# Attention: two triangles of weights added and transposed as one

## The chip, the cores and the metric

The kernel runs on one core of a Trainium2 chip. The core has a matmul engine (TensorE, PE in the profile, with its weight loads as PEld), a vector engine (VectorE, DVE), a scalar engine (ScalarE, ACT), a general one (GpSimd, POOL) and SyncE (SP), which issues nearly all DMAs here. Each takes its instructions in order and they meet through semaphores. SBUF is the working memory and PSUM the banks into which TensorE accumulates. The metric is device time of one execution, in microseconds (us).

## The reference

Two layers of a hybrid decoder over 512 tokens of width 1024, all in fp32. Each layer normalises its input, makes one projection (queries, keys and values for attention; queries, keys, values and a gate for retention; two output gates), runs sliding-window attention and chunkwise retention side by side, merges both through the gates, projects, adds, and then does the same with an MLP (squared ReLU, width 4096). The part that matters:

```python
C = WINDOW                       # 128
kk, vv = band(kb), band(vb)      # the block of keys before, and the block itself
s = einsum('bnqhgd,bnkhd->bnhgqk', qb, kk) * HEAD_DIM ** -0.5
rel = (arange(C)[:, None] + C) - arange(2 * C)[None, :]
valid = (rel >= 0) & (rel < WINDOW)
s = where(valid & first, s, -inf)
p = softmax(concatenate([s, sink], -1), -1)[..., :-1]
o = einsum('bnhgqk,bnkhd->bnqhgd', p, vv)
```

There are 8 query heads in 2 groups, one group to each of 2 key-value heads. A block of 128 queries sees 256 keys. Query i sees key j of the block before only if j > i, and key j of its own block only if j <= i. So the weights that are not zero fill a strict upper triangle of the first 128x128 block and the lower triangle with the diagonal of the second: together exactly one full square. The first query block has no block before it.

## The kernel before

**Products.** Every fp32 operand of a large product is split into a high and a low part, each in a form that TensorE multiplies at full rate (fp32r), and a product is three matmuls: high by high, high by low, low by high (`products`, L297 to L299). The split is a copy on ScalarE and a subtraction on VectorE: L252 and L253 for weights, `split` (L304, L305) for everything else. Weights come by DMA as 128x1024 units in the order of use (L193); `unit` sees to it that while unit i is multiplied, i+1 and i+2 are being split, with three buffers for the parts. A unit is 24 matmuls of 512 columns.

**Order.** The code is traced in program order; a planner then places each engine's instructions in an order of its own by its own costs of instructions and its own times at which they are ready, and gives out the buffers. So program order is a priority, not the order in the queues, and the queues are fixed before the kernel runs.

**Attention** is a generator that runs in the background: `chunk` calls `advance` twice per unit, which does 0.8 of a step each time while the gates, the first retention queries and keys, and the first retention gates are being projected. A step takes one query block n and one pair c of heads (one head of each group g), 16 steps per layer. In a step:
- four score matmuls into one PSUM bank, `ps` (L669): 128 queries by w keys, w = 128 for n = 0 and 256 otherwise, for two heads side by side;
- scaling, masking and the row minimum in one VectorE instruction per head (L677), from `ps` to the SBUF tile `sm` (the signs are turned, so a minimum stands for the maximum), with `nsink`, the negated sinks made once at L288, as its start; then the sink's term (L687);
- exponentials with their row sums on ScalarE (L689, L692); masked weights become zero;
- sum and reciprocal on VectorE (L693, L694), and the scaling of all w weights of each head (L696);
- `transposed` for the step of three before (the queue `pend`): a transpose by TensorE of each 128x128 block of weights into a bank `pT` (L634), four for n > 0 and two for n = 0, and a split of the bank into `p_h` and `p_l`, from which the product with values reads.

`weighted(n)` runs two steps after the last `transposed` of block n: per group, two matmuls per key block (L654, L655; tile `pv`), then the two halves are joined (L656, L657) and split. Its result is first read by the product with w_a, some tens of us after attention ends. The tiles `sm` and the rotary temporaries share six buffers; `score`, `pT`, `pv` and others share three PSUM banks; main products have five.

**Start.** SP issues the first input, inputs and weights in turn, then the table `band` (the mask of attention, L280), further weights and the rotary tables. A small tile of constants sits in front of x in the tile `little_x`.

Of the kernel before, what the change touches and what calls it, by code (L numbers as in the profile page):

```python
# [14 lines left out]
ALU = mybir.AluOpType  # L15
# [3 lines left out]
P = 128  # L19
# [7 lines left out]
N_KV = 2  # L27
# [93 lines left out]


@with_exitstack
def decoder(ctx, tc, xT, x_first, w_in, w_a, w_b, w_out, w_up, w_down, tables, decay, band, g_last, out):
    nc = tc.nc
    weights = {"w_in": w_in, "w_a": w_a, "w_b": w_b, "w_out": w_out, "w_up": w_up, "w_down": w_down}

# [17 lines left out]
    def bank(pool, name):  # L145
        return pool.tile([P, T], F32, tag=pool.name, name=name)
# [4 lines left out]
    n_gain, n_sink = 2 * DEPTH * KD, DEPTH * N_Q  # L151
    little_x = const.tile([P, P + KD * T], F32, name="x")
    gain = little_x[:, P - n_gain : P]
    sink = little_x[:, P - n_gain - n_sink : P - n_gain]
    eps, half, nsink = (little_x[:, a : a + n] for a, n in ((0, 1), (8, N_KV), (16, n_sink)))
    x = little_x[:, P:].rearrange("p (k t) -> p k t", t=T)
    xhl = const.tile([P, 2, KD, T], F32R, name="xhl")
    xh, xl = xhl[:, 0], xhl[:, 1]
# [119 lines left out]

    mask = const.tile([P, 2 * P], F32, name="mask")
    nc.sync.dma_start(mask, band)  # L280

    ident = const.tile([P, P], F32, name="ident")
    make_identity(nc, ident)
    nc.gpsimd.memset(half, 0.0)
    for g in range(N_KV):
        for b in (0, 64):
            nc.gpsimd.memset(half[b + 32 * g : b + 32 * g + 32, g : g + 1], 1.0)
    nc.vector.tensor_scalar(nsink, sink, -1.0, None, ALU.mult)  # L288


    def products(ps, pairs, start, stop, resume=False):
# [206 lines left out]
    def layer_body(layer):  # L498
# [124 lines left out]
        def attention():  # L623
            p_t = [slots.four() for _ in range(2)]
            p_h, p_l = p_t[0][0], p_t[1][0]
            pend, ready = [], []

            def transposed(n, c, sm):
                w = P if n == 0 else 2 * P
                kbs = (1,) if n == 0 else (0, 1)  # L630
                pt = bank(ps_aux, "pT")
                for i, (g, kb) in enumerate((g, kb) for g in range(N_KV) for kb in kbs):
                    at = g * w + (kb - kbs[0]) * P
                    nc.tensor.transpose(pt[:, i * P : (i + 1) * P], sm[:, at : at + P], ident)  # L634
                m = 2 * len(kbs)
                src = pt[:, : m * P].rearrange("p (i q) -> p i q", q=P)
                first = kbs[0]
                hi = p_h[:, first :: 2 if n == 0 else 1, c * P : (c + 1) * P]
                lo = p_l[:, first :: 2 if n == 0 else 1, c * P : (c + 1) * P]
                split(hi, lo, src)  # L640

            def weighted(n):
                at = slice(n * P, (n + 1) * P)
                both = big("whole")
                rest, whole = both[:, 0, :], both[:, 1, :]
                for g in range(N_KV):
                    own, other = slice(64 * g, 64 * g + 64), slice(64 - 64 * g, 128 - 64 * g)
                    po = bank(ps_aux, "pv")
                    kbs = (1,) if n == 0 else (0, 1)
                    for kb in kbs:  # L650
                        b = n - 1 + kb
                        cols = slice(b * P, (b + 1) * P)
                        p = 2 * g + kb
                        nc.tensor.matmul(po, v_both[g][:, cols], p_h[:, p, :], start=kb == kbs[0], stop=False)  # L654
                        nc.tensor.matmul(po, v_high[g][:, cols], p_l[:, p, :], start=False, stop=kb == 1)  # L655
                    nc.scalar.activation(rest[own, :], po[other, :], AF.Copy)  # L656
                    nc.vector.tensor_tensor(whole[own, :], po[own, :], rest[own, :], ALU.add)  # L657
                split(a_h[:, :, at], a_l[:, :, at], whole.rearrange("p (c q) -> p c q", q=P))

            for n in range(NB):  # L660
                w = P if n == 0 else 2 * P
                keys = slice(0, P) if n == 0 else slice((n - 1) * P, (n + 1) * P)
                at = slice(n * P, (n + 1) * P)
                for c in range(4):
                    col = layer * N_Q + 2 * c
                    ps = bank(ps_aux, "score")
                    for g in range(N_KV):
                        for i, part in enumerate((kh[g], kl[g])):
                            nc.tensor.matmul(  # L669
                                ps[:, g * w : (g + 1) * w], q_s[g][:, c, at], part[:, keys], start=i == 0, stop=i == 1  # L670
                            )
                    sm = temp("sm")
                    s3 = sm[:, : 2 * w].rearrange("p (g k) -> p g k", g=2)
                    st = small.tile([P, 8], F32, tag="st", name="st")
                    nm, es, su, rc = (st[:, 2 * i : 2 * i + 2] for i in range(4))
                    for g in range(N_KV):
                        nc.vector.tensor_tensor_reduce(  # L677
                            s3[:, g, :],
                            ps[:, g * w : (g + 1) * w],
                            mask[:, 2 * P - w :],  # L680
                            -(HEAD_DIM**-0.5),
                            nsink[:, col + g : col + g + 1],
                            ALU.add,
                            ALU.min,
                            nm[:, g : g + 1],
                        )
                    nc.vector.tensor_tensor(es, nm, sink[:, col : col + 2], ALU.add)  # L687
                    for g in range(N_KV):
                        nc.scalar.activation(  # L689
                            s3[:, g, :], s3[:, g, :], AF.Exp, bias=nm[:, g : g + 1], scale=-1.0, accum_out=su[:, g : g + 1]  # L690
                        )
                    last_exp[:] = [nc.scalar.activation(es, es, AF.Exp).ins]  # L692
                    nc.vector.tensor_tensor(rc, su, es, ALU.add)  # L693
                    nc.vector.reciprocal(rc, rc)  # L694
                    for g in range(N_KV):
                        nc.vector.tensor_scalar(s3[:, g, :], s3[:, g, :], rc[:, g : g + 1], None, ALU.mult)  # L696
                    pend.append((n, c, sm))
                    if ready and c == 1 + DELAY:
                        weighted(ready.pop())
                    if len(pend) > DEEP:  # L700
                        done = pend.pop(0)
                        transposed(*done)
                        if done[1] == 3:
                            ready.append(done[0])
                    yield
            while pend:
                transposed(*pend.pop(0))
                yield
            weighted(NB - 1)
            for t in q_t + p_t:  # L710
                slots.give(*t[1])
            slots.give(*k_s, *v_s)
# [198 lines left out]
        for u in range(4):  # L911
            hi, lo = unit("w_a", layer)
            for j in range(2):
                c = 2 * u + j
# [394 lines left out]
def _tables():  # L1309

    f = np.float32
    pos = np.arange(T, dtype=f)
    inv = np.power(10000.0, -np.arange(32) / 32).astype(f)
    ang = pos[None, :] * np.tile(inv, 4)[:, None]
    sign = np.where(np.arange(P) < 64, f(-1), f(1))[:, None]
    steps = np.append(np.arange(63, dtype=f) * (f(1) / f(63)), f(1))
    theta = f(1.0) / np.power(10000.0, steps.astype(np.float64)).astype(f)
    ang_r = pos[None, :] * np.tile(theta, 2)[:, None]
    rotary = np.stack([np.cos(ang), sign * np.sin(ang), np.cos(ang_r), sign * np.sin(ang_r)], 1).astype(f)

    log_g = np.log(1.0 - 2.0 ** (-5.0 - np.arange(RET_HEADS)))
    rel = np.arange(T)[None, :] - np.arange(P)[:, None]
    decay = np.where(rel[:, None, :] >= 0, np.exp(log_g[None, :, None] * np.maximum(rel, 0)[:, None, :]), 0.0)
    decay = (decay * RET_QK**-0.5).astype(f)

    rel = np.arange(P)[:, None] + P - np.arange(2 * P)[None, :]
    band = np.where((rel >= 0) & (rel < P), f(0), f(MASKED)).astype(f)
    return rotary, decay, band


def _laid_out(x, g_mix, w_in, sinks, w_a, w_b, w_out, g_mlp, w_up, w_down, g_final):
    r = np.arange
    wa_rows = np.concatenate([(4 * g + c) * HEAD_DIM + r(HEAD_DIM) for c in range(4) for g in range(2)])
    rotary, decay, band = _tables()
    gains = np.stack([g for l in range(DEPTH) for g in (g_mix[l], g_mlp[l])])
    heads = np.array([4 * g + c for c in range(4) for g in range(2)])
    xT = np.ascontiguousarray(x[0].T.reshape(KD, P, T).transpose(1, 0, 2))
# [11 lines left out]
        "tables": rotary,  # L1349
        "decay": decay,  # L1350
        "band": band,
        "g_last": np.ascontiguousarray(np.broadcast_to(g_final, (P, D))),
    }

# [17 lines left out]
```

## Time and profile before

| | |
|---|---|
| median of 3 runs | 1494.0 us (1493.49 to 1494.09) |
| profiled execution | 1494.36 us, of which the span from first to last instruction is 1492.6 us |
| granted TensorE clock | 0.999 |
| TensorE busy | 1485.9 us, 7212 matmuls |
| VectorE busy | 1063.4 us, 1709 instructions |
| ScalarE busy | 757.5 us, 1212 instructions |
| transposes of weights (L634) | 112, started between 61.8 and 866.0 us |

How to read it: the page of the profile gives busy time per engine, then the chain that ended last, which follows from the last instruction back to whatever released each one. A group line gives line, engine, operation, output and inputs with their shapes, count, then busy us and the mean ns of one, then the idle time of that engine ahead of them and what ended it. In a timeline the first number is the start and the second the duration, of all of a merged run together. A duration is that of one instruction from its start to its end; TensorE overlaps neighbours, so what a matmul costs the stream is the distance to the next start. Attention of layer 0 lies at about 50 to 150 us, that of layer 1 at about 785 to 880.

### The profile page before, as it was taken

How to read it: one execution, taken by the hardware profiler on the slowest of the kernel's cores; microseconds unless marked ns; L12 is line 12 of the kernel's file. 1: busy time of each engine (PE TensorE's matmuls, PEld its weight loads, DVE VectorE, ACT ScalarE, POOL GpSimd, SP SyncE). 2: the span in 40 equal slices, each digit the busy share in tenths (PEclk: the TensorE clock that was granted, in tenths of full speed). 3: DMA queues.
4: the chain of work that ended last, by engine and by line, in shares of the span. 5: the costliest groups of instructions: out<-in, count | busy, mean ns of one | idle time of the engine just before them, and what ended most of it. 6: DMA issues, size and time to landing. Idle time of an engine off the chain costs nothing.

```text
span 1492.6 us, 19003 instructions
## 1 busy us (share of the span) xinstructions
PE 1485.9 (100%) x7212; PEld 1253.3 (84%) x7212; DVE 1063.4 (71%) x1709; ACT 757.5 (51%) x1212; POOL 2.9 (0%) x13
## 2 busy tenths in 40 slices
PE   9999999999999999999999999999999999999998
PEld 7888888888888888888888888888888888888887
DVE  7877568754688787777678864687448877787763
ACT  6657355533555545444455653546326554454543
POOL 0000000000000000000000000000000000000000
PEclk9999999999999999999999999999999999999999
DMA  6422323244323332324442323232443232333341
GB/s 223 125 93 72 97 87 91 73 120 122 105 78 111 102 101 91 112 92 131 161 129 89 97 76 97 85 92 71 127 127 100 80 103 85 113 113 104 95 141 57
DMA packets 51835, 155.53 MB, mean 104 GB/s; under 512 B 6176, under 2 KB 6304, under 8 KB 51744
## 3 DMA queue, kind: packets, MB, share of 16 engines
q1 hardware_dynamic: 51456, 153.80, 33.9%
q8 instruction: 56, 0.92, 0.2%
q10 hardware_dynamic: 288, 0.52, 0.1%
q14 instruction: 35, 0.29, 0.1%
HBM read 147.48 MB, written 4.19 MB: 102 GB/s over the span
## 4 chain that ended last, share of the span: by engine, by line
PE 100%; DVE 0%; ACT 0%; issue 0%; DVEq 0%; ACTq 0%
PE mm L297 23%; PE mm L298 23%; PE mm L299 23%; PE mm L1096 11%; PE mm L1097 6%; PE rv L297 2%; PE rv L299 2%; PE rv L298 2%; PE score L669 1%; PE pT L634 1%; PE r L298 1%; PE r L299 1%; PE r L297 1%; PE pv L654 0%; PE pv L655 0%; PE ssq L394 0%
## 5 line engine op out<-in xcount | busy, mean ns | idle before, releaser
L252 ACT ACTIVATE hi<-raw 128x1024 fp32r<-128x1024 f32 (+1 forms) x314 | 316.9, 1013 | 461.4 <-PE mm L298 274.6
L253 DVE TENSOR_TENSOR lo<-raw,hi 128x1024 fp32r<-128x1024 f32 (+1 forms) x315 | 365.7, 1165 | 177.4 <-ACT hi L252 176.6
L298 PE MATMUL mm<-r,hi 128*128 128x512 f32 (+1 forms) x704 | 271.1, 385 | 0.0
L297 PE MATMUL mm<-xhl,hi 128*128 128x512 f32 (+1 forms) x696 | 269.8, 390 | 0.0
L297 PE MATMUL mm<-r,hi 128*128 128x512 f32 (+1 forms) x704 | 269.5, 386 | 0.0
L298 PE MATMUL mm<-xhl,hi 128*128 128x512 f32 (+1 forms) x696 | 268.6, 388 | 0.0
L299 PE MATMUL mm<-xhl,lo 128*128 128x512 f32 (+1 forms) x696 | 267.6, 388 | 0.0
L299 PE MATMUL mm<-r,lo 128*128 128x512 f32 (+1 forms) x704 | 266.6, 385 | 0.0
L299 PEld LDWEIGHTS mm<-r,lo 128*128 128x128 f32 x704 | 132.2, 188 | 26.6
L298 PEld LDWEIGHTS mm<-r,hi 128*128 128x128 f32 x704 | 132.3, 188 | 25.6
L297 PEld LDWEIGHTS mm<-r,hi 128*128 128x128 f32 x704 | 131.8, 188 | 26.0 <-DVE z L1075 0.3
L297 PEld LDWEIGHTS mm<-xhl,hi 128*128 128x128 f32 x696 | 131.0, 188 | 25.1 <-ACT xhl L307 0.8
L299 PEld LDWEIGHTS mm<-xhl,lo 128*128 128x128 f32 x696 | 130.9, 188 | 24.9
L298 PEld LDWEIGHTS mm<-xhl,hi 128*128 128x128 f32 x696 | 131.0, 188 | 24.3
L1096 PE MATMUL mm<-r,hi 128*128 128x512 f32 x416 | 146.8, 391 | 0.0
L1097 PE MATMUL mm<-r,lo 128*128 128x256 f32 x416 | 115.6, 278 | 0.0
L1096 PE MATMUL mm<-xhl,hi 128*128 128x512 f32 x312 | 110.5, 391 | 0.0
L1096 PEld LDWEIGHTS mm<-r,hi 128*128 128x128 f32 x416 | 78.2, 188 | 16.2
L1097 PE MATMUL mm<-xhl,lo 128*128 128x256 f32 x312 | 86.7, 278 | 0.0
L1097 PEld LDWEIGHTS mm<-r,lo 128*128 128x128 f32 x416 | 78.1, 188 | 1.8
L1096 PEld LDWEIGHTS mm<-xhl,hi 128*128 128x128 f32 x312 | 58.6, 188 | 11.8
L1097 PEld LDWEIGHTS mm<-xhl,lo 128*128 128x128 f32 x312 | 58.6, 188 | 1.7
(229 smaller groups left out, 2069.9 us busy)
## 6 DMA issues: line engine op xcount, KB each, us to landing
raw<-w_in_in SPq DMA_DIRECT2D x89, 512.0 KB, 3.6
raw<-w_down_in SPq DMA_DIRECT2D x64, 512.0 KB, 3.6
raw<-w_up_in SPq DMA_DIRECT2D x36, 512.0 KB, 3.6
raw<-w_up_in SPq DMA_DIRECT2D x56, 256.0 KB, 2.7
raw<-w_b_in SPq DMA_DIRECT2D x16, 512.0 KB, 3.6
raw<-w_out_in SPq DMA_DIRECT2D x16, 512.0 KB, 3.9
raw<-w_a_in SPq DMA_DIRECT2D x8, 512.0 KB, 3.5
x<-xT_in SPq DMA_DIRECT2D x15, 256.0 KB, 3.8
```

The costliest lines, as they stand in the source:

```text
L252: nc.scalar.activation(hi[:, at], raw[:, at], AF.Copy)
L253: last_low[:] = [nc.vector.tensor_tensor(lo[:, at], raw[:, at], f32(hi[:, at]), ALU.subtract).ins]
L297: nc.tensor.matmul(ps, ah, bh, start=start and i == 0, stop=False, **more)
L298: nc.tensor.matmul(ps, ah, bl, start=False, stop=False, **more)
L299: nc.tensor.matmul(ps, al, bh, start=False, stop=stop and i == n - 1, **more)
L634: nc.tensor.transpose(pt[:, i * P : (i + 1) * P], sm[:, at : at + P], ident)
L669: nc.tensor.matmul(ps[:, g * w : (g + 1) * w], q_s[g][:, c, at], part[:, keys], start=i == 0, stop=i == 1)
L1096: nc.tensor.matmul(both, hi[:, c], m, start=start and k == 0, stop=False, **more)
L1097: nc.tensor.matmul(ps[:, :H], lo[:, c], m[:, 0, :], start=False, stop=k == 3 and start, **more)
```

## The change

For query blocks with two key blocks (n > 0), the weights of both are added in place after the exponentials: each element of the sum has one term that is not zero. Only the sum, 128 columns per head, is scaled by the reciprocal and transposed, so a step has two transposes. VectorE then multiplies the transposed square in PSUM by two masks, one triangle of ones and its complement, reading each square twice and writing both results side by side into the same `sm` tile (which the transposes have read by then). The split takes its source from there rather than from PSUM. The masks are bytes, 128x256, loaded by a new DMA from a new input into 64 columns of the small constants' tile, where `nsink` was; the sinks are negated in place instead, and the sink's term is taken by a subtraction. Block n = 0 is as it was.

```diff
-    eps, half, nsink = (little_x[:, a : a + n] for a, n in ((0, 1), (8, N_KV), (16, n_sink)))
+    eps, half, keep = (little_x[:, a : a + n] for a, n in ((0, 1), (8, N_KV), (16, P // 2)))
+    keep = keep.bitcast(mybir.dt.uint8)
...
     nc.sync.dma_start(mask, band)
+    nc.sync.dma_start(keep, triangles)
...
-    nc.vector.tensor_scalar(nsink, sink, -1.0, None, ALU.mult)
+    nc.vector.tensor_scalar(sink, sink, -1.0, None, ALU.mult)
...
             def transposed(n, c, sm):
                 w = P if n == 0 else 2 * P
-                kbs = (1,) if n == 0 else (0, 1)
                 pt = bank(ps_aux, "pT")
-                for i, (g, kb) in enumerate((g, kb) for g in range(N_KV) for kb in kbs):
-                    at = g * w + (kb - kbs[0]) * P
-                    nc.tensor.transpose(pt[:, i * P : (i + 1) * P], sm[:, at : at + P], ident)
-                m = 2 * len(kbs)
-                src = pt[:, : m * P].rearrange("p (i q) -> p i q", q=P)
-                first = kbs[0]
-                hi = p_h[:, first :: 2 if n == 0 else 1, c * P : (c + 1) * P]
-                lo = p_l[:, first :: 2 if n == 0 else 1, c * P : (c + 1) * P]
+                for g in range(N_KV):
+                    nc.tensor.transpose(pt[:, g * P : (g + 1) * P], sm[:, g * w : g * w + P], ident)
+                src = pt[:, : 2 * P].rearrange("p (g q) -> p g q", q=P)
+                first, step = (1, 2) if n == 0 else (0, 1)
+                hi = p_h[:, first::step, c * P : (c + 1) * P]
+                lo = p_l[:, first::step, c * P : (c + 1) * P]
+                if n > 0:
+                    both = sm.rearrange("p (g b q) -> p g b q", b=2, q=P)
+                    every = [P, N_KV, 2, P]
+                    apart = keep.rearrange("p (b q) -> p b q", q=P).unsqueeze(1).broadcast_to(every)
+                    nc.vector.tensor_tensor(both, src.unsqueeze(2).broadcast_to(every), apart, ALU.mult)
+                    src = sm.rearrange("p (i q) -> p i q", q=P)
                 split(hi, lo, src)
...
-                            nsink[:, col + g : col + g + 1],
+                            sink[:, col + g : col + g + 1],
...
-                    nc.vector.tensor_tensor(es, nm, sink[:, col : col + 2], ALU.add)
+                    nc.vector.tensor_tensor(es, nm, sink[:, col : col + 2], ALU.subtract)
...
+                    if n > 0:
+                        nc.vector.tensor_tensor(s3[:, :, :P], s3[:, :, :P], s3[:, :, P:], ALU.add)
                     for g in range(N_KV):
-                        nc.vector.tensor_scalar(s3[:, g, :], s3[:, g, :], rc[:, g : g + 1], None, ALU.mult)
+                        nc.vector.tensor_scalar(s3[:, g, :P], s3[:, g, :P], rc[:, g : g + 1], None, ALU.mult)
...
+    before = np.arange(P)[None, :] < np.arange(P)[:, None]
+    triangles = np.concatenate([before, ~before], 1).astype(np.uint8)
```

More of the change, by code (lines that the diff above doesn't have):

```diff
@@ L123, in decoder @@
 @with_exitstack
-def decoder(ctx, tc, xT, x_first, w_in, w_a, w_b, w_out, w_up, w_down, tables, decay, band, g_last, out):
+def decoder(ctx, tc, xT, x_first, w_in, w_a, w_b, w_out, w_up, w_down, tables, decay, band, triangles, g_last, out):
     nc = tc.nc
@@ L1327, in _tables @@
     band = np.where((rel >= 0) & (rel < P), f(0), f(MASKED)).astype(f)
-    return rotary, decay, band
+    before = np.arange(P)[None, :] < np.arange(P)[:, None]
+    triangles = np.concatenate([before, ~before], 1).astype(np.uint8)
+    return rotary, decay, band, triangles
 def _laid_out(x, g_mix, w_in, sinks, w_a, w_b, w_out, g_mlp, w_up, w_down, g_final):
@@ L1333, in _laid_out @@
     wa_rows = np.concatenate([(4 * g + c) * HEAD_DIM + r(HEAD_DIM) for c in range(4) for g in range(2)])
-    rotary, decay, band = _tables()
+    rotary, decay, band, triangles = _tables()
     gains = np.stack([g for l in range(DEPTH) for g in (g_mix[l], g_mlp[l])])
@@ L1351, in _laid_out @@
         "band": band,
+        "triangles": triangles,
         "g_last": np.ascontiguousarray(np.broadcast_to(g_final, (P, D))),
```

## The prediction

> **What bounds the kernel now.** I read the page first: busy times, granted clock and the chain that ended last.
>
> ```profile
> span 1492.6 us, 19003 instructions
> ...
> PE 1485.9 (100%) x7212; PEld 1253.3 (84%) x7212; DVE 1063.4 (71%) x1709; ACT 757.5 (51%) x1212; POOL 2.9 (0%) x13
> ...
> PEclk9999999999999999999999999999999999999999
> ...
> PE 100%; DVE 0%; ACT 0%; issue 0%; DVEq 0%; ACTq 0%
> ```
>
> TensorE (PE) is busy all the time, at full clock, and the chain is TensorE from end to end. A busy row can hide waiting, since ends of matmuls are modelled, so I read the list of waits next: TensorE's own first, then the largest of ScalarE (ACT).
>
> ```profile
> PE warm L277 <- DVE ones L272: 1.1, 1, 1.1
> ```
>
> ```profile
> ACT hi L252 <- PE mm L298: 274.6, 93, 4.8
> ```
>
> In 1492.6 us TensorE waited once, 1.1 us at the start. The others wait for it: ScalarE stands 274.6 us until TensorE is done with a weight buffer. So the time is the sum of what TensorE issues, as long as VectorE (DVE), ScalarE and the DMAs keep their lead. The change takes work from TensorE and gives work to VectorE, so two questions decide: what does a transpose cost in TensorE's stream, and does VectorE keep its lead?
>
> The view of the tile pT shows what is touched:
>
> ```profile
> L634 PE MATMUL pT<-ident,sm x112: 269/272/300, 61.8 to 866.0; 128*128 128x128 f32 x112
> L304 ACT ACTIVATE r<-pT x32: 362/598/600, 62.2 to 866.3; 128x512 fp32r<-128x512 f32 x24, 128x256 fp32r<-128x256 f32 x8
> L305 DVE TENSOR_TENSOR r<-pT,r x32: 415/684/693, 62.6 to 867.2; 128x512 fp32r<-128x512 f32 x24, 128x256 fp32r<-128x256 f32 x8
> ```
>
> 112 transposes: 24 units (a query block with a pair of heads, both layers together) with four each, and 8 units of the first query block with two. The change leaves those 8 alone and halves the 24: 48 transposes go.
>
> **Transposes removed (TensorE).** The 272 ns of one are latency; what counts is the distance between starts, from the timeline of TensorE:
>
> ```profile
> 70.29 0.38 PE L634 MATMUL pT<-ident,sm 128*128 128x128 f32 x2
> 70.42 0.48 PE L298 MATMUL mm<-xhl,hi 128*128 128x512 f32 x1
> 70.74 0.39 PE L299 MATMUL mm<-xhl,lo 128*128 128x512 f32 x1
> ...
> 84.03 0.60 PE L634 MATMUL pT<-ident,sm 128*128 128x128 f32 x4
> 84.39 0.48 PE L297 MATMUL mm<-xhl,hi 128*128 128x512 f32 x1
> 84.70 0.39 PE L298 MATMUL mm<-xhl,hi 128*128 128x512 f32 x1
> ...
> 865.22 1.04 PE L634 MATMUL pT<-ident,sm 128*128 128x128 f32 x8
> ```
>
> Two transposes hold the stream for 0.13 us (70.29 to 70.42), four for 0.36 (84.03 to 84.39). The product behind them takes 0.31 or 0.32 to the next one, after two as after four, where a product elsewhere takes 0.23: that is the price of a run, and it stays. The slope is (0.36 - 0.13) / 2 = 0.11 us per transpose; eight in a row say the same, being 0.27 for one and 1.04 for all: (1.04 - 0.27) / 7 = 0.11. 48 x 0.11 = 5.3 us off TensorE's stream. The lowest price that I find for 128 columns in this stream is that of two score products, which hold it for 0.17 us:
>
> ```profile
> 52.28 0.34 PE L669 MATMUL score<-r,r 128*128 128x128 f32 x2
> 52.45 0.45 PE L298 MATMUL mm<-xhl,hi 128*128 128x512 f32 x1
> ```
>
> At 0.085 each the 48 would bring 4.1 us. I take 0.11, since it is of the same instruction.
>
> The Trainium skill (TensorE: Matmul & The Clock Gate, section "Back-to-back issue gap") gives 134 cycles at 2.4 GHz for 128 columns, which is 56 ns; by that estimate the 48 would bring 2.7 us and the time be about 1491.3. The trace differs: eight in a row stand 0.11 us apart.
>
> **The add, the narrower scaling, the masked multiply (VectorE), the split (both).** Prices come from the groups with shapes kept apart:
>
> ```profile
> L305 DVE TENSOR_TENSOR r<-rot,r 128x512 fp32r<-128x512 f32 x16 | 10.9, 681 | 7.8 <-ACT r L304 7.8
> L1107 DVE TENSOR_TENSOR eu<-eu 128x256 f32<-128x256 f32 x26 | 10.9, 421 | 1.2 <-ACT eu L1126 0.4
> L696 DVE TENSOR_SCALAR sm<-sm,st 128x256 f32<-128x256 f32 x48 | 14.6, 349 | 0.5
> L696 DVE TENSOR_SCALAR sm<-sm,st 128x128 f32<-128x128 f32 x16 | 3.9, 283 | 0.2
> L304 ACT ACTIVATE r<-rot 128x512 fp32r<-128x512 f32 x16 | 10.0, 627 | 7.3 <-DVE rot L520 7.2
> L253 DVE TENSOR_TENSOR lo<-raw,hi 128x1024 fp32r<-128x1024 f32 x281 | 343.4, 1223 | 174.4 <-ACT hi L252 173.6
> L396 DVE RECIPROCAL inv<-inv 128x512 f32<-128x512 f32 x8 | 26.8, 3352 | 12.2 <-ACT inv L395 12.2
> ```
>
> Per unit of the 24: the add of two blocks, 128x256 in SBUF, +0.42 us (L1107's form). Two scalings of 128 columns in place of 256, -2 x 0.07. The multiply by the mask of bytes, 128x512 from PSUM: no row has a byte operand. The nearest is the subtraction from PSUM, at 0.68 to 0.69 in the view of pT; the far ends are 0.42 (half the elements) and 3.35 (the slowest 128x512 of VectorE). I take 0.69. The split's subtraction then reads SBUF instead of PSUM: 681 ns against the median of 684 in the view of pT, nothing; ScalarE's copy goes from 598 (pT's view) to 627 ns, 24 x 0.03 = 0.7 us on an engine that is busy 51%. Sum on VectorE: 0.42 - 0.14 + 0.69 = 0.97 us per unit, 11.6 us per layer, none of it on the path while the lead holds.
>
> For the byte operand the Trainium skill (VectorE: DVE Perf Modes, section "Specifications") says that integer operands are converted and computed as fp32; no run here shows it.
>
> **Does the lead hold?** Time by stretches, all engines, then VectorE's work on pT alone in the same stretches, of which each of 128x512 marks a unit that I charge with the whole 0.97:
>
> ```profile
> 801.00:834.00 33.00, 33.00 (x167) 27.88 (x166) 25.96 (x81) 18.48 (x50) 0.00 (x0) 1.00 0.29 95
> 834.00:857.00 23.00, 23.00 (x119) 19.28 (x118) 21.29 (x57) 16.90 (x36) 0.00 (x0) 1.00 0.25 72
> 857.00:868.00 11.00, 11.00 (x58) 9.23 (x57) 8.02 (x12) 9.36 (x14) 0.00 (x0) 1.00 0.28 90
> 868.00:880.00 12.00, 12.00 (x57) 9.92 (x56) 6.83 (x9) 4.37 (x8) 0.00 (x0) 1.00 0.25 69
> ...
> 110.00:120.00 10.00, 10.00 (x57) 8.63 (x56) 9.30 (x30) 8.24 (x22) 0.00 (x0) 1.00 0.31 100
> ```
>
> ```profile
> 801.00:834.00 33.00, 3.58 (x6) 1.00 0.29 95
> 834.00:857.00 23.00, 2.74 (x4) 1.00 0.25 72
> 857.00:868.00 11.00, 2.57 (x4) 1.00 0.28 90
> ...
> 110.00:120.00 10.00, 2.03 (x3) 1.00 0.31 100
> ```
>
> The columns of the first are PE, PEld, DVE, ACT. In layer 1, VectorE is idle 7.04 us of the first stretch (four units: two of the six are of the first query block, 3.9 us to add), 1.71 of the second (3.9), 2.98 of the third (3.9), 5.17 of the fourth (none: the last subtraction on pT starts at 867.2). So it falls 2.2 us behind by 857, 3.1 by 868, and has caught up by 880. How late may it be? Weights are what TensorE needs from it soonest. Three buffers go round, and while unit i is multiplied i+1 and i+2 are being split; so the low part of i+2, begun at the start of i, has two periods, less copy and subtraction. The period is that between gate evacuations:
>
> ```profile
> 824.22 0.69 DVE L729 TENSOR_TENSOR x<-mm,rstd 128x512 f32<-128x512 f32 x1 [1.10 <-PE mm L299]
> 831.45 0.69 DVE L729 TENSOR_TENSOR x<-mm,rstd 128x512 f32<-128x512 f32 x1
> ...
> 865.96 1.88 DVE L305 TENSOR_TENSOR r<-pT,r 128x512 fp32r<-128x512 f32 x3
> ```
>
> ```profile
> 871.12 0.39 PE L654 MATMUL pv<-r,r 128*128 128x512 f32 x1
> ```
>
> 2 x 7.2 = 14.4, less 1.2 for the subtraction (L253) and at most 1.3 for the copy (twice the 0.63 of 512 columns), is 12 us of lead, against 3.1 us of lateness. Layer 0's fullest stretch, the last row of both fences, has 0.70 us idle and three units, 2.9 us to add: 2.2 late.
>
> **New waits.** ScalarE's copy now waits for VectorE's multiply, which waits for the transposes; behind the copy on ScalarE stand exponentials and the copies of weights, which the 12 us cover. The product with the values waits for transposes, multiply, copy and subtraction: now the last subtraction ends at 867.84 and the product starts at 871.12, 3.3 us spare, against 0.69 more chain and the lateness of up to 3.1. That is tight; a planner that orders TensorE by its own costs can put main products ahead of it, so I charge nothing; uncovered it is the first rival. The score tile stays in use until its split instead of its transposes: six buffers, four of them held by units in flight; a rotation may wait some 2 us (0.69 + 0.63 + 0.68) for one, behind which only an evacuation waits, with five accumulators.
>
> **The mask's DMA (SP).** One more issue of 32 KB behind that of the band, and a small negation done in place:
>
> ```profile
> 8.84 0.33 SPq L280 DMA_DIRECT2D mask<-band_in  x1
> 9.59 0.33 SPq L193 DMA_DIRECT2D raw<-w_in_in  x1
> ```
>
> The queue is free from 9.17 to 9.59, and one issue takes 0.33: nothing. Its first reader is at about 84 us. Missing the hole, it makes one load 0.4 us late, inside the weights' lead.
>
> **Sum.** -48 x 0.11 = -5.3 us. The profiled execution took 1494.36 us (span 1492.6), 0.36 above the median of the runs: it would become 1489.1, and the median 1494.0 becomes 1488.7, -0.35%. What a measurement can tell from no change is 0.2%, 3.0 us.
>
> **Rivals.** (a) Waiting takes the gain: the product with the values stands for its longer chain. Price: three query blocks per layer, 6 waits, each 0.69 + 3.1 - 3.3 = 0.5 us if the spare is kept and VectorE is at its latest, 0.7 if the planner uses up the spare and VectorE is on time (0.69 of the multiply, 0.03 of the slower copy): 3.0 to 4.2 us, so 1491.7 to 1492.9. For it: nothing reorders TensorE's queue at run time. Against it: the same queue has not waited once for VectorE after the start. (b) The saving is smaller: a run that is halved pays something again, at most once more the 0.09 of a run's end (0.32 - 0.23): 24 x 0.09 = 2.2 us, so 1490.9. For it: a run of 0.13 us covers less of the weight loads around it. Against it: the runs of two that are there already pay 0.32 behind them, as those of four do. The page's gap named above gives a like time by another way, which the eight in a row speak against. (c) Slower: the masked multiply, L305's neighbour on VectorE, runs far off the 0.69. In layer 1 the lateness is 12 x (price + 0.28) - 11.7, the idle time of its first three stretches, and it reaches the 12 us of lead at a price of 1.7 us. At the far end, 3.35, it is 32 us, 20 of them TensorE's, and with as much in layer 0 the time is 1494.0 - 5.3 + 40 = 1529. Slower than before by 3 us it is from 2 x (12 x (price + 0.28) - 23.7) = 8.3 on, a price of 2.0. For it: a byte operand stands in no row. Against it: the two-input forms of 128x512 quoted above take 0.68 to 0.69. (d) The change does not do what it says, and four transposes stay: excluded, since the new loop runs over the two key groups only.
>
> **How the numbers follow.** Forecast 0.84 (1487.2 to 1490.5, whose ends are a few runs more or fewer, each 0.09, and the score's price of 0.085); (a) 0.07; (b) 0.03, which I count as within 0.2%, for it is at the border; (c) 0.06. Faster 0.84, same 0.07 + 0.03 = 0.10, slower 0.06. The range reaches from 1487.0 to 1492.0: it takes in the forecast's own, (b) and the lighter end of (a); out stay the heavier end of (a) and (c).
>
> **What would show it.** Right: 64 transposes in place of 112, runs of two at 0.13 us, TensorE's list of waits still with nothing of VectorE or ScalarE, VectorE near 1087 us busy with a multiply group x24 near 0.69. Wrong: a wait of TensorE on VectorE or ScalarE in 100 to 150 or 830 to 880 us; a multiply of over 1.7 us; low parts of weights that end just ahead of their first product.

## The result and the profile after

The median went from 1493.97 us (1493.49 to 1494.09) to 1488.67 us (1488.07 to 1489.28), six runs each: a ratio of 0.9964 [0.9954, 0.9974], 5.3 us faster. The forecast was 1488.7. The profiled execution took 1488.07 us, 0.60 below the median; that of before stood 0.36 above its own.

The page of the kernel after: span, busy times, granted clock, and the shares of the chain that ended last.

```profile
span 1486.3 us, 18956 instructions
...
PE 1479.6 (100%) x7164; PEld 1247.5 (84%) x7164; DVE 1081.0 (73%) x1757; ACT 760.0 (51%) x1212; POOL 2.9 (0%) x13
...
PEclk9999999999999999999999999999999999999999
...
PE 100%; DVE 0%; ACT 0%; issue 0%; DVEq 0%; ACTq 0%
```

TensorE is as full as before and has 48 matmuls fewer; VectorE has 48 instructions and 17.6 us more. Whether VectorE's extra work touches TensorE is read from the waits. TensorE's whole list, then the largest of ScalarE (total us, times, longest):

```profile
PE warm L278 <- DVE ones L273: 1.1, 1, 1.1
```

```profile
ACT hi L253 <- PE mm L300: 270.8, 95, 4.8
```

TensorE waits for nobody after the start, and ScalarE still stands 270.8 us for TensorE's weight buffers (274.6 before). The direction of waiting has not turned. The view of the tile pT and, from the timeline of TensorE, one of its runs:

```profile
L637 PE MATMUL pT<-ident,sm x64: 270/272/299, 58.7 to 865.7; 128*128 128x128 f32 x64
...
L646 DVE TENSOR_TENSOR sm<-pT,x x24: 666/684/692, 78.9 to 867.2; 128x512 f32<-128x512 f32 x24
```

```profile
857.60 0.38 PE L637 MATMUL pT<-ident,sm 128*128 128x128 f32 x2
857.73 0.48 PE L299 MATMUL mm<-xhl,hi 128*128 128x512 f32 x1
858.05 0.39 PE L300 MATMUL mm<-xhl,hi 128*128 128x512 f32 x1
```

There are 64 transposes in place of 112, and a run of two holds the stream for 0.13 us with 0.32 behind it, as the runs of two did before. The masked multiply is there 24 times, at a median of 0.684 us. The groups of the added and changed work, shapes kept apart:

```profile
L307 DVE TENSOR_TENSOR r<-sm,r 128x512 fp32r<-128x512 f32 x24 | 16.2, 684 | 0.3
L646 DVE TENSOR_TENSOR sm<-pT,x 128x512 f32<-128x512 f32 x24 | 16.1, 686 | 0.7 <-PE pT L637 0.3
L706 DVE TENSOR_SCALAR sm<-sm,st 128x128 f32<-128x128 f32 x64 | 15.0, 281 | 0.4
...
L704 DVE TENSOR_TENSOR sm<-sm 128x256 f32<-128x256 f32 x24 | 10.1, 421 | 2.7 <-ACT sm L697 2.3
...
L306 ACT ACTIVATE r<-sm 128x512 fp32r<-128x512 f32 x24 | 14.8, 624 | 15.3 <-DVE sm L646 15.2
```

**Span and medians.** The profiled span fell by 6.3 us, the medians by 5.3. Most of that difference of 1.0 us lies at the start, in work of TensorE that the change leaves as it was. The first rows of TensorE's timeline, before and then after:

```profile
1.05 4.63 PE L277 MATMUL warm<-ones 128*128 128x512 f32 x10 [1.05 <-DVE ones L272]
...
5.73 1.35 PE L297 MATMUL mm<-xhl,hi 128*128 128x512 f32 x4
```

```profile
1.05 4.32 PE L278 MATMUL warm<-ones 128*128 128x512 f32 x10 [1.05 <-DVE ones L273]
...
5.21 1.16 PE L299 MATMUL mm<-xhl,hi 128*128 128x512 f32 x4
```

The ten warm-up matmuls took 4.63 us in the one execution and 4.32 in the other, and the first four products end at 7.08 and 6.37: 0.7 us that has nothing to do with attention. This is why the sum goes by the medians.

### The profile page after: what moved, and what is told of

Its sections match the earlier page's. It is cut to its first block, busy times and chain, and to the rows that moved or that the text cites. A ratio compares the mean times of both kernels' runs of the same rounds, so it can differ in the third digit from the quotient of the medians.

```text
span 1486.3 us, 18956 instructions
## 1 busy us (share of the span) xinstructions
PE 1479.6 (100%) x7164; PEld 1247.5 (84%) x7164; DVE 1081.0 (73%) x1757; ACT 760.0 (51%) x1212; POOL 2.9 (0%) x13
## 4 chain that ended last, share of the span: by engine, by line
PE 100%; DVE 0%; ACT 0%; issue 0%; DVEq 0%; ACTq 0%
PE mm L299 24%; PE mm L300 23%; PE mm L301 23%; PE mm L1106 11%; PE mm L1107 6%; PE rv L299 2%; PE rv L300 2%; PE rv L301 2%; PE score L677 1%; PE r L301 1%; PE r L300 1%; PE r L299 1%; PE pT L637 0%; PE pv L663 0%; PE pv L662 0%; PE ssq L396 0%
## 5 line engine op out<-in xcount | busy, mean ns | idle before, releaser
L253 ACT ACTIVATE hi<-raw 128x1024 fp32r<-128x1024 f32 (+1 forms) x314 | 316.8, 1013 | 451.5 <-PE mm L300 270.8
L300 PE MATMUL mm<-r,hi 128*128 128x512 f32 (+1 forms) x704 | 270.8, 385 | 0.0
```

The source lines that it names most:

```text
L253: nc.scalar.activation(hi[:, at], raw[:, at], AF.Copy)
L300: nc.tensor.matmul(ps, ah, bl, start=False, stop=False, **more)
```

## Experiments

The theory: the whole gain is what 48 transposes cost in TensorE's stream, and VectorE's added work is free because it lies inside the lead that VectorE has, that is, the time by which its results are ready before TensorE needs them. The rivals: part of the gain comes from elsewhere or part of the cost is hidden by chance (a wait avoided, a run's fixed price), or the lead is nearly used up. The first four runs take the change apart; the other six shorten the lead until it breaks, and ask where.

### The transposes alone

Two transposes more per step, into columns of the bank that nobody reads:

```diff
                 for g in range(N_KV):
                     nc.tensor.transpose(pt[:, g * P : (g + 1) * P], sm[:, g * w : g * w + P], ident)
+                    if n > 0:
+                        nc.tensor.transpose(pt[:, (2 + g) * P : (3 + g) * P], sm[:, g * w : g * w + P], ident)
```

> The changed kernel with two more transposes per step of two key blocks, of the same two blocks, into the unused half of the bank pT, where nothing reads them: 112 transposes again, all else as changed. If the gain is the 48 transposes in TensorE's stream at 0.11 us each, it goes: 1488.7 + 5.3 = 1494.0 us, runs of four at 0.36 us. If the gain came from another order of the queues or from VectorE's new arrangement, the time stays at 1488.7 to 1490.

1494.16 us (1493.69 to 1495.05), a ratio to before of 1.0001 [0.9992, 1.0010]. The gain is gone, though everything else of the change is in place. From its page:

```profile
PE 1484.9 (100%) x7212; PEld 1252.5 (84%) x7212; DVE 1081.1 (72%) x1757; ACT 760.0 (51%) x1212; POOL 2.9 (0%) x13
```

Against the kernel after, TensorE is 5.3 us busier for 48 matmuls, 0.11 each; by the medians it is 5.5 us, 0.114 each. So the 48 transposes carry the gain, at the price that the slope gave.

### VectorE's work alone

The kernel before, with its four transposes, and beside them an operation of 128x256 on `sm` in place (the larger of a block and itself, which changes nothing) and a multiply of the bank by a table of bytes, all ones, whose result is not read:

```diff
+    table = little_x[:, 40:72].bitcast(mybir.dt.uint8)
+    nc.vector.memset(little_x[:, 40:72].bitcast(mybir.dt.uint32), 0x01010101)
...
+                if n > 0:
+                    whole = sm.rearrange("p (i q) -> p i q", q=P)
+                    nc.vector.tensor_tensor(whole, src, table.unsqueeze(1).broadcast_to([P, 4, P]), ALU.mult)
...
+                    if n > 0:
+                        nc.vector.tensor_tensor(s3[:, :, :P], s3[:, :, :P], s3[:, :, :P], ALU.max)
```

> The kernel before with VectorE's added work alone: per step of two key blocks a two-input instruction of 128x256 in place (the larger of a block and itself) and a multiply of 128x512 from pT into the score tile by a table of byte ones, which nothing reads; four transposes and the split from PSUM stay. If VectorE's 11 to 12 us per layer lie wholly beside TensorE, the time is that of before, 1494.0 (within 1 us). If they eat into the lead, it is 1495 to 1500, with waits of TensorE.

1494.12 us (1493.88 to 1494.44), ratio 1.0000 [0.9990, 1.0009]. From its page:

```profile
PE 1484.9 (100%) x7212; PEld 1252.4 (84%) x7212; DVE 1083.8 (73%) x1758; ACT 758.9 (51%) x1212; POOL 2.9 (0%) x13
```

20.4 us more on VectorE than before, and no time. Here the subtraction on pT does not depend on the multiply, so this shows that VectorE's time is hidden, not that the longer chain is.

### Without the multiply

The kernel after without the masks: the split reads the bank twice directly, so both key blocks get the whole square.

```diff
-                    both = sm.rearrange("p (g b q) -> p g b q", b=2, q=P)
                     every = [P, N_KV, 2, P]
-                    apart = keep.rearrange("p (b q) -> p b q", q=P).unsqueeze(1).broadcast_to(every)
-                    nc.vector.tensor_tensor(both, src.unsqueeze(2).broadcast_to(every), apart, ALU.mult)
-                    src = sm.rearrange("p (i q) -> p i q", q=P)
+                    src = src.unsqueeze(2).broadcast_to(every)
+                    hi, lo = (t.rearrange("p (g b) q -> p g b q", b=2) for t in (hi, lo))
```

> The changed kernel without the multiply by the masks: the split reads each transposed square twice straight from PSUM, so the weights of both key blocks are their sum and the attention output is another one. If the multiply is hidden, the time stays at 1488.7 (within 1 us), with VectorE about 16 us less busy. If the longer chain of transpose, multiply, copy and subtraction costs something, the time falls by 1 to 4 us, to 1485 to 1488.

1488.55 us (1488.45 to 1488.70), ratio 0.9964 [0.9950, 0.9977], as the kernel after to 0.1 us. From its page:

```profile
PE 1479.9 (100%) x7164; PEld 1247.3 (84%) x7164; DVE 1067.7 (72%) x1733; ACT 759.2 (51%) x1212; POOL 2.9 (0%) x13
```

VectorE is 13.3 us less busy, and the chain to the product with the values is a multiply shorter. Neither brings anything: both are hidden in the kernel after.

### Two steps in one run

If a run of transposes has a fixed price at its end, as the prediction read the rows, then fewer runs should bring more. The transposes of two steps go into one bank, one after the other; each half of the bank is then multiplied and split as before:

```diff
+            def transposed_two(two):
+                pt = bank(ps_aux, "pT")
+                for i, (n, c, sm) in enumerate(two):
+                    w = P if n == 0 else 2 * P
+                    for g in range(N_KV):
+                        at = (2 * i + g) * P
+                        nc.tensor.transpose(pt[:, at : at + P], sm[:, g * w : g * w + P], ident)
...
-                    if len(pend) > DEEP:
-                        done = pend.pop(0)
-                        transposed(*done)
+                    if len(pend) > DEEP and c % 2:
+                        two = [pend.pop(0), pend.pop(0)]
+                        transposed_two(two)
```

> The changed kernel with the transposes of two steps put into one bank, one run of four in place of two runs of two. If the 0.09 us that the first product behind a run pays belongs to the run and not to the transposes, 16 runs fewer are 1.4 us: 1487.3. If it belongs to each transpose, or the order of the planner splits the runs again, no change: 1488.7.

1488.94 us (1488.26 to 1489.32), ratio 0.9966 [0.9953, 0.9978]: nothing gained. Its timeline of TensorE has 18 runs of transposes in place of 32; at 0.09 each the 14 that are gone would have brought 1.3 us. One of the joined runs:

```profile
853.61 0.60 PE L636 MATMUL pT<-ident,sm 128*128 128x128 f32 x4
853.96 0.48 PE L299 MATMUL mm<-xhl,hi 128*128 128x512 f32 x1
854.28 0.40 PE L300 MATMUL mm<-xhl,hi 128*128 128x512 f32 x1
```

From the run's start to the second product behind it are 0.67 us, one product of 0.23 and 0.44 of transposes: 0.11 each. For the run of two shown above (857.60 to 858.05) it is 0.45 less 0.23, 0.22: again 0.11 each. So a run has no price of its own, and a run of four that is cut to two pays nothing extra. The 0.09 behind a run belongs to its transposes: it shows up in the step of the product that follows.

### How far the lead goes: the multiply two, three and five times

```diff
-                    nc.vector.tensor_tensor(both, src.unsqueeze(2).broadcast_to(every), apart, ALU.mult)
+                    for _ in range(2):
+                        nc.vector.tensor_tensor(both, src.unsqueeze(2).broadcast_to(every), apart, ALU.mult)
```

> The changed kernel with the masked multiply issued twice (the same result written again), 1.3 us per step on VectorE. By the prediction's lead (12 us; lateness 12 x (price + 0.28) - 11.7 in layer 1, crossing at 1.7 us), nothing: 1488.7 within 1 us. If the lead is shorter than reckoned, 1490 to 1495.

> The changed kernel with the masked multiply issued three times, 1.9 to 2.1 us per step. By the prediction's lead the crossing is passed: 3 to 5 us of TensorE's waiting, 1492 to 1494. If the planner spreads attention over more of the layer instead (its result is wanted some tens of us later), nothing: 1488.7 to 1490, with the last transposes later.

> The changed kernel with the masked multiply issued five times, 3.0 to 3.4 us per step, some 27 to 32 us more per layer. By the prediction's lead 25 to 37 us of waiting: 1514 to 1526. If the planner spreads attention, far less: 1489 to 1497, VectorE full between 800 and 900 us.

| multiplies | median us | against after | ratio to before |
|---|---|---|---|
| 0 | 1488.55 (1488.45 to 1488.70) | -0.1 | 0.9964 [0.9950, 0.9977] |
| 1 | 1488.67 (1488.07 to 1489.28) | | 0.9964 [0.9954, 0.9974] |
| 2 | 1491.10 (1490.59 to 1492.71) | +2.4 | 0.9981 [0.9972, 0.9991] |
| 3 | 1499.77 (1498.97 to 1501.43) | +11.1 | 1.0039 [1.0024, 1.0054] |
| 5 | 1539.62 (1538.14 to 1539.78) | +51 | 1.0301 [1.0284, 1.0318] |

All three miss what the prediction's lead gave (1488.7, 1492 to 1494, 1514 to 1526): the loss sets in earlier and grows faster. The lead ends between one multiply and two. TensorE's list of waits, with two:

```profile
PE pv L663 <- ACT r L306: 1.7, 1, 1.7
...
```

with three:

```profile
PE pv L663 <- ACT r L306: 4.1, 2, 2.5
PE rv L300 <- DVE lo L254: 1.3, 1, 1.3
...
PE pv L664 <- DVE r L307: 0.6, 1, 0.6
```

The first to wait is pv, the product with the values, for the split of the weights of attention: L663 reads the high part, ScalarE's copy, and L664 the low part, VectorE's subtraction. With three multiplies 1.3 us of 6.0 are the low part of a weight; the rest is pv. With five there are 36.7 us of waits after the start: 16.8 are pv's, and 18.5 are transposes and scores that wait for VectorE.

The waits of 6.0 us do not make 11.1. The rest is in the granted clock: the view by windows of the run with three, around the wait of 2.5 us (columns: length, PE, PEld, DVE, ACT and POOL busy with counts, granted clock, DMA share, GB/s):

```profile
128.00:130.00 2.00, 0.73 (x6) 0.49 (x4) 2.00 (x5) 1.92 (x5) 0.00 (x0) 1.00 0.57 229
130.00:132.00 2.00, 0.80 (x2) 0.70 (x3) 2.00 (x6) 1.98 (x7) 0.00 (x0) 0.81 0.02 4
132.00:134.00 2.00, 1.40 (x4) 0.74 (x4) 2.00 (x7) 0.61 (x4) 0.00 (x0) 0.50 0.49 96
134.00:136.00 2.00, 2.00 (x6) 1.56 (x5) 2.00 (x7) 1.99 (x2) 0.00 (x0) 0.50 0.44 174
136.00:138.00 2.00, 2.00 (x6) 1.52 (x6) 2.00 (x6) 2.00 (x2) 0.00 (x0) 0.50 0.00 0
```

After the wait TensorE runs at half its clock for some 6 us; in the next window the clock is 0.99 again. In these 6 us TensorE is busy 5.4 (1.40 + 2.00 + 2.00), so 2.7 us are lost, and up to 0.4 (0.19 x 2) in the window before: some 3 us, for waits of 2.5 and 0.6. The two waits of layer 1 lower the clock too, though neither is longer than 1.7 us; they end at 889.0 and 892.1, and then:

```profile
892.00:894.00 2.00, 1.93 (x7) 1.69 (x8) 2.00 (x4) 0.10 (x2) 0.00 (x0) 0.60 0.03 10
894.00:896.00 2.00, 2.00 (x6) 1.51 (x6) 0.53 (x2) 0.89 (x3) 0.00 (x0) 0.55 0.00 0
```

That is another 1.7 us (0.40 x 2 + 0.45 x 2). The page of this run gives the total:

```profile
PE 1485.6 (99%) x7164; PEld 1250.4 (83%) x7164; DVE 1107.6 (74%) x1805; ACT 759.2 (51%) x1212; POOL 2.9 (0%) x13
```

The same 7164 matmuls kept TensorE busy 6.0 us longer than in the kernel after, and 6.0 of waits make it 12.0 of the 12.1 between the two profiled executions (1500.19 and 1488.07). Some 0.6 of such a difference in busy time is there without any wait (1480.2 in the run with three in the last block alone, below). With five the mean granted clock is 0.985, TensorE is 14.8 us busier, and 36.7 of waits make it 51.5, which is the whole difference. The run with two shows how a shorter wait goes; its windows around the 1.7 us, at 146.9 to 148.6:

```profile
146.00:148.00 2.00, 0.94 (x5) 0.43 (x3) 2.00 (x5) 0.73 (x2) 0.00 (x0) 1.00 0.71 184
148.00:150.00 2.00, 1.41 (x8) 1.24 (x9) 1.90 (x4) 0.71 (x2) 0.00 (x0) 1.00 0.19 78
```

The clock stays. 1.7 of waiting cost 2.4 by the medians, and 2.5 by the profiled executions.

### Which block's product: three multiplies in the last block only, or in the others only

With three multiplies everywhere pv stands twice: for the third query block of layer 0, up to 131.2 us, and for the last block of layer 1, behind the wait for a weight. TensorE's timeline there:

```profile
889.01 0.50 PE L300 MATMUL rv<-lo,xhl 128*128 128x512 f32 x1 [1.34 <-DVE lo L254]
...
892.07 0.95 PE L663 MATMUL pv<-r,r 128*128 128x512 f32 x2 [1.64 <-ACT r L306]
```

If the spare ahead of the last block's product is too small by itself, tripling that block's multiplies alone should bring its wait back; if lateness comes from earlier blocks, these matter.

```diff
-                    nc.vector.tensor_tensor(both, src.unsqueeze(2).broadcast_to(every), apart, ALU.mult)
+                    for _ in range(3 if n == NB - 1 else 1):
+                        nc.vector.tensor_tensor(both, src.unsqueeze(2).broadcast_to(every), apart, ALU.mult)
```

The other run has the 1 and the 3 the other way round.

> The multiply three times as in the run before, but only in the four steps of the last query block of each layer; the other blocks have it once. That is a third of the added work, 4 x 1.2 us per layer, and it stands just ahead of the last product with the values. If what breaks is that product's wait for its chain, most of the loss at the last blocks comes back: 1490 to 1496, with a wait of that product in both layers. If it is the total that VectorE falls behind against the lead of the weights, a third of the work is well inside it: 1488.7 to 1489.5.

> The multiply three times in the second and third query block, once in the last: two thirds of the added work, further from the end of attention. If the product with the values waits for its chain, only that of the third block may wait: 1489 to 1494. If VectorE's total counts, two thirds of the loss: 1495 to 1497.

Last block only: 1488.73 us (1488.31 to 1489.16), ratio 0.9963 [0.9949, 0.9977], no loss at all, where a wait of that product was to bring 1490 to 1496. TensorE's waits hold only the one at the start. The timelines of VectorE and TensorE show how near it is in layer 0:

```profile
144.75 1.89 DVE L307 TENSOR_TENSOR r<-sm,r 128x512 fp32r<-128x512 f32 x3
```

```profile
146.62 0.62 PE L663 MATMUL pv<-r,r 128*128 128x512 f32 x2
147.43 0.47 PE L664 MATMUL pv<-r,r 128*128 128x512 f32 x1
```

The last subtraction ends at 146.64; the first matmul that reads a low part starts at 147.43, 0.8 us later. Here the order that the planner wrote has room for the two added multiplies.

The others only: 1495.42 us (1494.62 to 1496.81), ratio 1.0010 [1.0000, 1.0019]: 6.7 of the 11.1 us. Its waits:

```profile
PE pv L663 <- ACT r L306: 2.5, 1, 2.5
...
PE pv L664 <- DVE r L307: 0.6, 1, 0.6
```

These are the waits of the third block in layer 0, 2.5 + 0.6 = 3.1 us; behind them the granted clock falls much as above, and TensorE is 3.6 us busier than in the kernel after (1483.2 for 1479.6). That is 6.7 of the 6.8 between the profiled executions (1494.89 and 1488.07). So the larger part of the 11.1 us comes from one place. The time lies in the range given for VectorE's total lateness, but the waits are those of the other case, the third block's product, at a higher price than was put there; no weight is among them. The waits in layer 1 are there only when all blocks are tripled: neither the last block alone nor the others alone bring them. That fits a lateness of VectorE that is carried from block to block, but it is not shown, because the planner writes another order for each kernel. With two multiplies everywhere it is the last block of layer 0 that waits, at a place where three bring none:

```profile
148.59 0.73 PE L663 MATMUL pv<-r,r 128*128 128x512 f32 x2 [1.65 <-ACT r L306]
```

### The last product later

The last block's product is asked for two steps of the generator later, with three multiplies everywhere:

```diff
+            yield
+            yield
             weighted(NB - 1)
```

> The multiply three times in all steps (1499.8 us), and the last product with the values two half units of projection later in program order. If that product's wait is the loss, the part that comes from the last blocks goes: 1491 to 1496. If VectorE's lateness reaches TensorE through the weights, the time stays at 1498 to 1500.

1496.60 us (1495.27 to 1497.33), ratio 1.0015 [1.0005, 1.0024]: 3.2 of the 11.1 us come back. The waits of pv that are left:

```profile
PE pv L663 <- ACT r L306: 2.5, 1, 2.5
PE pv L664 <- DVE r L307: 1.2, 1, 1.2
```

Both waits of layer 1 are gone, pv's and that for the weight, and the third block's stay, since its product was not moved. So where the product stands in TensorE's queue can decide between a wait and none; the planner also wrote a new order here, so the move is not isolated from it. Why the planner leaves enough room ahead of one such product and not of another stays open: its own costs are in no trace.

## Why the prediction came out right, step by step

**Transposes, 48 x 0.11 = 5.3 us:** right, in size and in cause. The medians fell by 5.3; the run with four transposes again gives 0.114 each by the medians and 0.11 by TensorE's busy time. The 0.085 of the score products does not fit. Neither does the 0.056 us of the Trainium skill (TensorE: Matmul & The Clock Gate, section "Back-to-back issue gap"): that section calls it the isolated gap, and the 81 ns that it gives there for a stream of weight loads and matmuls is short of 0.11 too. Rival (b), that a halved run pays something more, falls: 0.13 and 0.32 in the rows after as before.

**"The price of a run, and it stays":** wrong, though it cost nothing. The joined runs brought no gain where this reading promises one, and two runs of different length both come to 0.11 per transpose once the product behind them is counted at 0.23. The rows quoted in the prediction say it already (70.29 to 70.74 less 0.23 is 0.22; 84.03 to 84.70 less 0.23 is 0.44). A slope between two lengths is safe against this; the price of a whole run read from its own start to the next start is not.

**VectorE's instructions:** each came out as priced. The add was put at 0.42 and measures 0.421, the narrower scaling 0.281 for 0.349, the multiply 0.686 for the 0.69 taken from the subtraction, and the copy on ScalarE 0.624 for 0.627. The multiply's row settles the widest unknown, whose far end was 3.35: rival (c)'s condition, a slow multiply, did not occur. The statement of the Trainium skill (VectorE: DVE Perf Modes, section "Specifications") that integer operands are converted and computed as fp32 fits the row, where a mask of bytes takes the time of an fp32 operand. Only the total was off, 1081.0 busy where some 1087 was expected. The step at fault is adding durations: neighbours on VectorE overlap. The run without the multiply has 13.3 us less for 24 of them, or 0.55 of busy time each, and on the timeline after three multiplies take 1.89 us together and not 3 x 0.69 = 2.07:

```profile
866.01 1.89 DVE L646 TENSOR_TENSOR sm<-pT,x 128x512 f32<-128x512 f32 x3
...
869.55 1.29 DVE L307 TENSOR_TENSOR r<-sm,r 128x512 fp32r<-128x512 f32 x2
```

So the charge of 0.97 per unit, and with it the lateness of 2.2 and 3.1 us, was a little on the high side.

**The product with the values, "tight, I charge nothing":** right that it does not wait, but the spare was misread. The first matmul of the product (L654 before, L662 after) reads only the high part, which is ScalarE's copy; the subtraction is needed first by the matmul behind it (L655, L663). The copies and the first product with a low part, before:

```profile
865.85 1.09 ACT L304 ACTIVATE r<-pT 128x512 fp32r<-128x512 f32 x2 [0.30 <-PE pT L634]
```

```profile
872.25 0.39 PE L655 MATMUL pv<-r,r 128*128 128x512 f32 x1
```

and after, with the first product:

```profile
868.22 1.14 ACT L306 ACTIVATE r<-sm 128x512 fp32r<-128x512 f32 x2
```

```profile
873.06 0.62 PE L662 MATMUL pv<-r,r 128*128 128x512 f32 x2
874.18 0.39 PE L663 MATMUL pv<-r,r 128*128 128x512 f32 x1
```

Before, the copy is done at 866.94 and the product starts at 871.12, 4.2 us later; the low part has 4.4 (867.84 to 872.25). The prediction's 3.3 set the end of the subtraction against a matmul that does not read it. With 4.2 in place of 3.3, the 0.69 of chain and 3.1 of lateness fit, so rival (a) was priced too high for this product. After, the spares are 3.7 (869.36 to 873.06) and 3.3 (870.84 to 874.18). The product starts 1.9 us later than before, though TensorE has some 5 us of transposes less to do ahead of it, so more of other work stands in front of it; left at 871.12 it would have had 1.8 us. That is the reason given for charging nothing, and the rows bear it out. It is also why rival (a) did not happen. But the planner's order was not worked out beforehand, and that it left room everywhere was in part luck: with one more multiply per step a product waits.

**The lead of 12 us and the crossing at 1.7 us:** wrong. The prediction took the weights as the first thing that TensorE would miss, and so put the first wait at a multiply of 1.7 us and the loss of 3 us against before at 2.0. Two multiplies, 2 x 0.69 less the overlap or some 1.3 us, bring a wait already; three, some 1.9 us, bring 11.1 us where this step gives about 5. What failed is the choice of the lead: in five of the six runs, all but that with the last block alone, the product with the values waits longest in total, and its spare, named under "New waits", was not carried into rival (c). The low part of a weight waits 1.3 us with three multiplies and 0.4 with five. The price of a wait was also too low, since it left out the clock. The 3.35 of the far end would have cost 40 us by the prediction, and 3.1 some 34; five multiplies, some 3.1 us, cost 51.

**SP, "nothing":** right in time, wrong in detail. The timeline of SP's queue after:

```profile
10.07 0.33 SPq L281 DMA_DIRECT2D mask<-band_in  x1
10.75 0.33 SPq L282 DMA_DIRECT2D x<-triangles_in  x1
11.49 0.33 SPq L194 DMA_DIRECT2D raw<-w_in_in  x1
```

The hole from 9.17 to 9.59 was not there in this execution. The band came 1.2 us later than before (10.07 for 8.84), and the load of weights followed it by 1.42 us where it had followed by 0.75: 0.7 us is the masks' share of a load that starts at 11.49 in place of 9.59. Of the two cases in the prediction it was the second, a load that is late, by 0.7 us for the masks and not 0.4. TensorE's list shows no wait for it.

## What to carry to other kernels

Price a removed instruction on a full engine by the slope between runs of different length; here it was right to 0.2 us in 1494. For work that is moved to another engine, look for the consumer with the least spare, which may be a small product in the middle of a background stage and not the stream of weights, and follow its chain instruction by instruction; the busy share (73% here) tells nothing of it. And ask which of its instructions reads which part: here the spare was misread by 0.9 us because the first matmul does not read what is finished last. A gain of 5 us stood on spares of 3 to 4 us in the queue's order: with one more multiply per step nearly half of it was gone, with two more the kernel was slower than before.

## What the hardware showed that was not expected

**A wait can cost twice.** A single wait of TensorE of 2.5 us was followed by a granted clock of 0.50 for some 6 us. Two waits of 1.34 and 1.64 us, with 1.4 us of work between them, brought it down to 0.60 and 0.55 over the next 4 us. One of 1.7 us alone left it at 1.00. In all, 3.1 us of waits cost 6.7. The Trainium skill (TensorE: Matmul & The Clock Gate, section "Why this matters for your kernels") warns of idle gaps above about 3 us; here 2.5 us was enough. The half clock agrees with the 4/8 that the Trainium skill gives (TensorE: Matmul & The Clock Gate, section "What's actually happening").

**Bytes are as cheap as fp32 on VectorE** in this form: 128x512 from PSUM times a broadcast mask of bytes took 0.686 us, the subtraction of two fp32 operands of the same shape 0.684.
